# A recurrent stage rewritten as streams put in order by an account of the engines' time

## The chip, the cores and the metric

The kernel runs on one NeuronCore of one Trainium2 chip. The metric is device microseconds of that core. The kernel before took 2466.32 us, the median of 3 runs (2462.35 to 2467.48). The profiled execution took 2471.44 us, and its span, on which all rows below lie, is 2469.7 us.

## The reference, cut to what matters

Two attention blocks come first and are not touched. The second block is an RWKV-7 time mix beside a causal convolution, then an FFN. x is 512 tokens by 1024 features; there are 16 heads of 64.

```
proj = rms_norm(x) @ w_in                     # 1024 x 7168: r, k, v, conv value and gate, two z gates
r, k, v = lerp_shift(p_r), lerp_shift(p_k), lerp_shift(p_v)
decay, a, g = small LoRAs of the shifted h
for t in range(512):                          # wkv7, per head, S is 64 x 64
    S = S * w_t + (S @ a_t) b_t^T + v_t k_t^T
    y_t = S @ r_t
y_rwkv = (groupnorm(y) + bonus) * g  @ w_rwkv_out
c = u * sigmoid(gate);  c = sum over 31 taps of dw[t] * c[time - t]      # depthwise, causal
y_conv = silu(layer_norm(c)) @ w_conv_out     # the norm runs over all 1024 channels
merged = sigmoid(z_rwkv) * y_rwkv + sigmoid(z_conv) * y_conv
x = x + rms_norm(merged @ w_out);  x = x + rms_norm(ffn(rms_norm(x)))
```

## The kernel before, in words

Every large product is done with fp32 operands split into a high and a low fp32r part. A weight tile arrives in `raw` (512 KB, two buffers, SP queue), ScalarE copies the high part `wh` (L160), VectorE subtracts to the low part `wl` (L161), and TensorE runs 8 matmuls each of wh by hT_h (L274), wh by hT_l (L275) and wl by hT_h (L277), all 128x512. Such a set of 24 is a dense unit here. The stage that the change rewrites runs from about 1277 to 2049 us and holds 72 dense units (1728 matmuls of 128x512): 24 for r, k and v, 16 for the convolution's input, 16 for the gates, and 16 for the two output maps.

The recurrence is done in chunks of 64 tokens, for 8 pairs of heads. Two pairs make a group, so there are 4 groups. The steps are

- `pair_in`: the three projections of a pair, and its LoRAs (tile `lo`).
- `pair_out`: decays, key norms, the products of the two heads inside each chunk (L1024, 64 rows by 128 columns), and transposes to tokens (L1040). POOL does r to the power -1/2 (L883).
- `solve`: the inverse of 1 minus a lower triangle of 64, for 32 chunks of a group. VectorE does 15 dependent steps on blocks of 16 (L1093, L1095), in two halves; then TensorE joins blocks of 16 to 32 with two sets of 64 matmuls of 32x32 (L1107, L1113), joins 32 to 64 (L1123, L1130), and applies the result (L1143). Blocks go through HBM in between (`abd`, `ttd`), issued by POOL.
- `chain`: 8 chunks one after the other: two products of the state (L1160, L1169), copies (L1171 ScalarE, L1172 VectorE), the new state (L1176, then L1179 on VectorE with `ds` from POOL, L1165), and the rest of y (L1182). All are 64x64.
- `post`: group norm of y, bonus and gate (L1192 to L1211).

The convolution of a feature tile is 30 VectorE instructions in a row (L1228, the taps). Layer norm needs all 8 tiles.

The order in which the steps are called is written out (`ORD`, L1259), but the order on every engine is made by the Tile framework's scheduler, with hand-set priority offsets `O`. Every engine then runs its instructions in that fixed order.

In the rows, `p` is a PSUM bank, SV the state and its products, X and RA the chunk matrices, BKT keys by token.

Of the kernel before, what the change touches and what calls it, by code (L numbers as in the profile page):

```python
# [72 lines left out]
def _constants():  # L73
# [3 lines left out]
    blk = np.concatenate([same, i[:, None] % 32 < 16, i[:, None] % 32 == np.arange(32),  # L77
                          (i[:, None] == i[None, :]) - same / 64], 1).astype(np.float32)
# [7 lines left out]

@with_exitstack
def tile_two_blocks(ctx: ExitStack, tc: tile.TileContext, A, out):
    nc = tc.nc
# [7 lines left out]
    make_identity(nc, ident)  # L97
# [27 lines left out]
    W["n"] = 0  # L125

# [24 lines left out]
    def wload(src, a, b, views=None, into=None):  # L151

        raw = W["raw"].tile([P, a, b], F32, tag="raw", name="raw")
# [4 lines left out]
        h, l = into or wpair(a, b)  # L158
# [447 lines left out]
    with ExitStack() as es:  # L606
# [206 lines left out]
        blk = pm.tile([P, 2 * P + 33], F32, name="blk")  # L813
# [21 lines left out]
        ahead = [wload(wcols(A["w_in_2"][0], 0, KD, i * D, P), KD, P,  # L835
# [27 lines left out]
    with ExitStack() as es:  # L863
        es.enter_context(lows)
# [4 lines left out]
        nc.vector.memset(smask[:, ::C], 0.0)  # L869
        two = blk[:, :P:64]  # L870
        i32 = blk[:, P + 1 : P + 33]
        centre = blk[:, P + 33 :]
        BANKS.update(ps=[0, 1, 2], po=[3, 4, 5], ca=[6], cb=[7], cc=[6, 7])

        def col_rstd(sq, rhs, eps, op, expand, role="po", scale=1.0):

            ps = pst(role)
# [3 lines left out]
            r = cs.tile([P, 8], F32, tag="r8" + role, name="r8")  # L881
            nc.vector.tensor_scalar(r, ps[:, :8], eps, None, op)
            nc.gpsimd.tensor_tensor(r, r, neg_half.to_broadcast([P, 8]), ALU.pow)  # L883
            nc.scalar.activation(expand.rearrange("p (t h d) -> p t h d", t=NB, h=2),
                                 r.rearrange("p (t h) -> p t h", h=2)[:, :, :, None].to_broadcast([P, NB, 2, 64]), AF.Copy, scale=scale)
            ps = pst(role)
# [7 lines left out]
        with ExitStack() as es2:  # L894
            el = es2.enter_context(tc.tile_pool(name="el", bufs=1))

            SH = 1

            def et(tag, n=T, bufs=1):
                return el.tile([P, n], F32, tag=tag, name=tag, bufs=bufs)  # L900

            def shifted(src, scale=None, **kw):

                sh = el.tile([P, T + 2], F32, tag="sh", name="sh", bufs=SH)
                nc.gpsimd.memset(sh[:, 0:1], 0.0)
# [342 lines left out]
            def at(offset, f, *a):  # L1248

                if not offset:  # L1250
                    return f(*a)
# [161 lines left out]
```

## Time and profile before

| what | value |
|---|---|
| median of 3 runs | 2466.32 us |
| profiled execution, and its span | 2471.44 us, 2469.7 us |
| TensorE busy (PE) | 2377.3 us, 96% |
| VectorE (DVE), ScalarE (ACT), GpSimd (POOL) busy | 51%, 38%, 12% |
| stage 1277 to 2049 us: PE, DVE, ACT, POOL busy of 772 us | 730.8, 565.8, 343.1, 198.5 |
| mean granted TensorE clock in that stage | 0.94 of 2.4 GHz |

PE is TensorE, PEld its weight loads. A busy engine is not an engine at its peak: in the plain FFN stage TensorE passes 223 matmuls of 128x512 in 50 us, and what it passes in the recurrent stage has to be read against that. A row of matmuls gives the time until the last result, so consecutive rows overlap; the distance from one start to the next is the price.

### The profile page before, as it was taken

The numbers are of one execution on the slowest core, as the hardware profiler recorded it, in microseconds if no ns is written. First come the engines' busy times: TensorE is split into PE (matmuls) and PEld (weight loads), VectorE is DVE, ScalarE is ACT, GpSimd is POOL, SyncE is SP. The second block draws the span as 40 slices with busy tenths as digits, with TensorE's granted clock in tenths as the row PEclk, the third lists the DMA queues.
The fourth block names the chain that finished last, engine by engine and source line by source line (L and its number), as shares of the span: only waits on it lengthen the run. The fifth ranks groups of instructions, "written<-read, shape, count | busy, mean of one in ns | idle before, by whom it ended". The sixth has DMA issues, their size and how long they took to land. (4 is left out here: it accounts for less than half of the span.)

```text
span 2469.7 us, 34315 instructions
## 1 busy us (share of the span) xinstructions
PE 2377.3 (96%) x13667; PEld 1869.2 (76%) x13667; DVE 1250.3 (51%) x2083; ACT 934.9 (38%) x1681; POOL 287.2 (12%) x455
## 2 busy tenths in 40 slices
PE   7899999999999999999999899999989999999998
PEld 6756888888887788888886676666667777888887
DVE  4376532143434642223446877588587764422232
ACT  4365432142344542222346344444344343422231
POOL 1000120000100000000012223233142101000000
PEclk9999999999999999999999999899799999999999
DMA  7320763143542263332232222123125454533321
GB/s 202 107 77 35 217 185 98 55 134 106 154 120 79 65 184 96 94 102 93 70 91 82 76 90 71 60 72 92 54 80 174 124 171 148 162 96 95 100 95 60
DMA packets 294240, 263.39 MB, mean 107 GB/s; under 512 B 13904, under 2 KB 260756, under 8 KB 293696
## 3 DMA queue, kind: packets, MB, share of 16 engines
q1 hardware_dynamic: 274648, 208.82, 28.3%
q0 software_dynamic: 10352, 30.02, 3.8%
q10 hardware_dynamic: 9080, 22.37, 3.0%
q8 instruction: 107, 1.75, 0.3%
q14 instruction: 53, 0.43, 0.1%
HBM read 226.33 MB, written 34.83 MB: 106 GB/s over the span
## 5 line engine op out<-in xcount | busy, mean ns | idle before, releaser
L274 PE MATMUL p<-hT_h,wh 128*128 128x512 f32 (+1 forms) x1776 | 686.7, 391 | 7.0 <-DVE cc L1218 3.3
L275 PE MATMUL p<-hT_l,wh 128*128 128x512 f32 (+1 forms) x1776 | 685.7, 390 | 0.0
L161 DVE TENSOR_TENSOR wl<-raw,wh 128x1024 fp32r<-128x1024 f32 (+2 forms) x348 | 410.8, 1184 | 424.5 <-ACT wh L160 360.2
L160 ACT ACTIVATE wh<-raw 128x1024 fp32r<-128x1024 f32 (+2 forms) x348 | 352.2, 1015 | 633.9 <-PE p L275 418.9
L277 PE MATMUL p<-hT_h,wl 128*128 128x512 f32 (+1 forms) x1776 | 449.1, 388 | 7.7 <-DVE wl L161 7.7
L274 PEld LDWEIGHTS p<-hT_h,wh 128*128 128x128 f32 x1776 | 340.3, 192 | 75.4 <-DVE cc L1218 4.5
L275 PEld LDWEIGHTS p<-hT_l,wh 128*128 128x128 f32 x1776 | 340.2, 192 | 66.1 <-issue 2.5
L277 PEld LDWEIGHTS p<-hT_h,wl 128*128 128x128 f32 x1776 | 322.4, 190 | 73.2 <-DVE wl L161 8.1
L168 PE MATMUL p<-wh,fh 128*128 128x512 f32 x528 | 206.1, 390 | 1.5 <-ACT memv L376 0.8
L169 PE MATMUL p<-wl,fh 128*128 128x512 f32 x528 | 205.9, 390 | 0.0
L170 PE MATMUL p<-wh,fl 128*128 128x512 f32 x528 | 205.2, 389 | 0.0
L1228 DVE SCALAR_TENSOR_TENSOR acc<-c,dwc,acc 128x512 f32<-128x512 f32 x240 | 186.0, 775 | 4.5
L300 DVE TENSOR_TENSOR fT<-sg,p 128x384 f32<-128x384 f32 (+1 forms) x88 | 46.8, 552 | 258.7 <-PE p L277 249.5
L192 POOL TENSOR_SCALAR rstd<-ss 128x1 f32<-128x1 f32 x24 | 9.2, 383 | 1445.6 <-ACT junk L188 1445.5
L175 DVE TENSOR_TENSOR fl<-fT,fh 128x512 fp32r<-128x512 f32 x66 | 45.1, 691 | 144.4 <-ACT fh L174 144.4
L168 PEld LDWEIGHTS p<-wh,fh 128*128 128x128 f32 x528 | 99.1, 188 | 23.0 <-ACT memv L376 1.2
L169 PEld LDWEIGHTS p<-wl,fh 128*128 128x128 f32 x528 | 99.1, 188 | 20.3
L170 PEld LDWEIGHTS p<-wh,fl 128*128 128x128 f32 x528 | 99.1, 188 | 20.3
L174 ACT ACTIVATE fh<-fT 128x512 fp32r<-128x512 f32 x66 | 40.8, 628 | 182.7 <-PE p L169 174.8
L168 PE MATMUL p<-wh,hT_h 128*128 128x256 f32 (+1 forms) x256 | 91.7, 359 | 2.6 <-ACT v L536 2.0
L169 PE MATMUL p<-wl,hT_h 128*128 128x256 f32 (+1 forms) x256 | 90.2, 353 | 0.6 <-DVE wl L161 0.6
L170 PE MATMUL p<-wh,hT_l 128*128 128x256 f32 (+1 forms) x256 | 89.0, 351 | 0.0
(328 smaller groups left out, 3053.5 us busy)
## 6 DMA issues: line engine op xcount, KB each, us to landing
raw<-in_w_gu SPq DMA_DIRECT2D x88, 512.0 KB
raw<-in_w_in SPq DMA_DIRECT2D x56, 512.0 KB
raw<-in_w_down SPq DMA_DIRECT2D x44, 512.0 KB
raw<-in_ffn_w_gate SPq DMA_DIRECT2D x22, 512.0 KB
raw<-in_ffn_w_up SPq DMA_DIRECT2D x22, 512.0 KB
raw<-in_ffn_w_down SPq DMA_DIRECT2D x22, 512.0 KB
raw<-in_w_in_b SPq DMA_DIRECT2D x20, 512.0 KB
xs<-xt POOLq DMA_DIRECT2D x19, 512.0 KB, 4.0
```

The costliest lines, as they stand in the source:

```text
L160: nc.scalar.activation(to(h), fr(raw), AF.Copy)
L161: nc.vector.tensor_tensor(to(l), fr(raw), to(h).bitcast(F32), ALU.subtract)
L168: nc.tensor.matmul(ps, lhsT=lh, rhs=rh, start=start, stop=False)
L169: nc.tensor.matmul(ps, lhsT=lh, rhs=rl, start=False, stop=False)
L170: nc.tensor.matmul(ps, lhsT=ll, rhs=rh, start=False, stop=stop)
L174: nc.scalar.activation(h, src, AF.Copy)
L175: nc.vector.tensor_tensor(l, src, h.bitcast(F32), ALU.subtract)
L274: nc.tensor.matmul(o[:, c], lhsT=h[:, k, :], rhs=hT_h[:, k, c], start=k == 0, stop=False)
L275: nc.tensor.matmul(o[:, c], lhsT=h[:, k, :], rhs=hT_l[:, k, c], start=False, stop=False)
L277: nc.tensor.matmul(o[:, c], lhsT=l[:, k, :], rhs=hT_h[:, k, c], start=False, stop=k == KD - 1)
L300: nc.vector.tensor_tensor(dst(fT[:, f, :]), src(sg), src(ps[1]), ALU.mult)
L1228: nc.vector.scalar_tensor_tensor(acc, c[:, t : t + T], dwc[:, t, f : f + 1], acc, ALU.mult, ALU.add)
```

## The change

The stage's code is rewritten as Python generators. Each `yield` marks a point at which the next instruction would have to wait. `Clock` keeps an account of each engine's time from fixed costs per instruction; `drive` walks through the dense units and lets each stream (two `pair_out` streams at once, `solve`, `chain`, `post`, the layer norm) emit its next burst when the account says that its inputs are ready. Bursts other than plain continuations wait for every eighth matmul of a dense unit. `Taps` fills VectorE's accounted idle time with convolution taps. TensorE and VectorE keep exactly the order in which the code emits; ScalarE, POOL and SP are still ordered by the framework.

Beside the order: the solve starts from blocks of 8 (7 dependent steps on VectorE, whole 128 rows at once) and joins 8 to 16 and 16 to 32 on TensorE with six sets of 64 matmuls in place of two; its trips through HBM are issued by SP and not by POOL; every second weight subtraction of the stage goes to POOL (36 of them); raw weights are fetched two units ahead; the merged result goes to hT in place of its own tiles.

```diff
+class Clock:
...
+    def cost(self, engine, op, out, ins):
+        n = max(math.prod(x.shape[1:]) for x in [out, *ins])
+        if op == "dma_start":
+            return 0.65 if engine == "POOL" else 0.05
+        if engine == "DVE":
+            return (0.21 if op == "scalar_tensor_tensor" else 0.14) + n * (0.00215 if op.endswith("scan") else 0.00107)
+        if engine == "ACT":
+            return 0.17 + n * 0.00086
...
+    def op(self, engine, op, out, ins, f, a, k):
+        need = max([self.ready(x) + 0.25 for x in ins] + [self.read.get(self.name(out), 0.0)])
+        if engine == "DVE" and self.fill is not None and not self.filling:
+            self.filling = True
+            self.fill(need)
+            self.filling = False
+        start = max(self.t[engine], need)
+        end = self.t[engine] = start + self.cost(engine, op, out, ins)
...
+    def until(self, t):
+        busy, self.clock.filling = self.clock.filling, True
+        while not self.done and self.clock.free("DVE") + 0.75 <= t:
+            got = next(self.gen, None)
...
-            nc.vector.tensor_tensor(to(l), fr(raw), to(h).bitcast(F32), ALU.subtract)
+            W["sub"][W["n"] % len(W["sub"])].tensor_tensor(to(l), fr(raw), to(h).bitcast(F32), ALU.subtract)
...
+        W["sub"] = [nc.vector, nc.gpsimd]
...
-                parts = (slice(0, 64), slice(64, P)) if g >= HALF else (slice(0, P),)
-                for t in range(1, 16):
...
+            for t in range(1, 8):
+                p4 = pr[:, : 2 * t * t].rearrange("p (m j s) -> p m j s", m=2, s=t)
+                nc.vector.tensor_tensor(p4, tt[:, :, :t, :t], at[:, :, None, :t, t].to_broadcast([P, 2, t, t]), ALU.mult)
+                nc.vector.tensor_reduce(tt[:, :, :t, t], p4, AX.X, ALU.add)
...
+            de = s2("de")
+            nc.scalar.activation(de, quad(of(e), of(dt), True), AF.Copy)
+            yield BURST
+            pa, pb = quad(of(de), of(dd)), quad(of(dd), of(de))
...
+            de = s2("de")
+            nc.scalar.activation(de, quad(lambda i: diag[i], of(dt), True), AF.Copy)
+            yield BURST
+            pb, pa = quad(of(dd), of(de)), quad(of(de), of(dd))
...
+        def drive():
+            streams = [[s, 0.0, None] for s in (chains(), outs(0), outs(1), solves(), posts(), ends())]
+            def burst(minor=False):
+                for s in list(streams):
+                    while s[1] <= clock.free("PE") and not (minor and s[2] in (BURST, FREE)):
+                        before = clock.free("PE")
+                        clock.last = 0.0
+                        got = s[2] = next(s[0], "end")
...
+                for n, minor in enumerate(run(hl) if run is not None else ()):
+                    if n == SPLIT and more:
+                        nxt, more = units[i + 1][1](raws.pop(0)), False
+                    burst(minor)
+                    taps.until(clock.free("PE") - 1)
...
+        with tc.manual_schedule(engines={mybir.EngineType.PE, mybir.EngineType.DVE}):
+            drive()
```

Every instruction that the wrapper `Timed` passes on stands in the changed program under one of three lines (L185, L191 on TensorE, L151 elsewhere), so its tiles name it.

The first place is TensorE at the start of the last group's chain. Before (SV, X, BKT, RA belong to the recurrence, hT and w to a dense unit, bk to another pair's products):

```order
L275 MATMUL p_14117<-hT_l,wh 128x512
L277 MATMUL p_14117<-hT_h,wl 128x512
L1160 MATMUL p_13789<-SV_12582,X_12581 64x64
L277 MATMUL p_14117<-hT_h,wl 128x512
L1160 MATMUL p_13789<-SV_12582,X_12581 64x64
L277 MATMUL p_14117<-hT_h,wl 128x512
L1024 MATMUL p_14268<-X_14068,bk 128x128
L1160 MATMUL p_13789<-SV_12582,X_12581 64x64
L277 MATMUL p_14117<-hT_h,wl 128x512
L1024 MATMUL p_14268<-X_14068,bk 128x128
L1160 MATMUL p_13789<-SV_12582,X_12581 64x64
L277 MATMUL p_14117<-hT_h,wl 128x512
```

The same kind of place in the changed program, one chunk of a chain between two dense stretches:

```order
L191 MATMUL p_12852<-hT_h,wh 128x512
L191 MATMUL p_12852<-hT_l,wh 128x512
L191 MATMUL p_12804<-SV_10548,BKT_10549 64x64 x4
L191 MATMUL p_12805<-RA_11268,SV_10548 64x64 x4
L191 MATMUL p_12886<-blk,RA_10181 128x2 x4
L191 MATMUL p_12893<-blk,RA_10181 128x2 x4
L191 MATMUL p_12852<-hT_h,wh 128x512
L191 MATMUL p_12852<-hT_l,wh 128x512
```

The four matmuls of a step now stand together, where they stood singly between dense ones.

The second place is VectorE in a group's solve. Before, its last steps (pr and tt are the solve, SV the chain, wl a weight's low part):

```order
L1093 TENSOR_TENSOR pr<-tt,at 64x169 x2
L1095 TENSOR_REDUCE tt<-pr 64x13 x2
L1172 COPY SV_11129<-p_12500 64x2x64
L161 TENSOR_TENSOR wl<-raw,wh 128x128
L1093 TENSOR_TENSOR pr<-tt,at 64x196 x2
L938 SCALAR_TENSOR_TENSOR rkv<-p_13195,der,sh 128x512
L1179 TENSOR_TENSOR SV_11129<-p_12501,ds 64x2x64 x2
L1095 TENSOR_REDUCE tt<-pr 64x14 x2
L1093 TENSOR_TENSOR pr<-tt,at 64x225 x2
L161 TENSOR_TENSOR wl<-raw,wh 128x1024
```

Now, the end of the second group's (x is the solve's scratch tile):

```order
L151 TENSOR_TENSOR x<-x 128x50
L151 TENSOR_REDUCE x<-x 128x2x5
L151 TENSOR_TENSOR x<-x 128x72
L151 TENSOR_REDUCE x<-x 128x2x6
L151 TENSOR_TENSOR x<-x 128x98
L151 TENSOR_REDUCE x<-x 128x2x7
L151 TENSOR_TENSOR wl<-raw,wh 128x1024
L151 TENSOR_TENSOR SV_9906<-p_11720,ds 64x2x64 x2
```

A solve has 14 such instructions where it had 60, and they stand in one block with nothing between them.

The third place is TensorE where the last chain ends. Before, the group norm of the last group (RA with blk, then ysq) stands among the matmuls of the first output map (X, SV with wh):

```order
L277 MATMUL p_15729<-hT_h,wl 128x512 x8
L1192 MATMUL p_15758<-RA_14071,blk 128x512
L1192 MATMUL p_15785<-RA_14071,blk 128x512
L879 MATMUL p_15763<-blk,ysq 128x2 x4
L1314 MATMUL p_15814<-X_15220,wh 128x512
L1315 MATMUL p_15814<-SV_15221,wh 128x512
```

Now, the last two chunks and the group norm stand with nothing dense between them:

```order
L191 MATMUL p_16494<-hT_h,wl 128x512 x8
L191 MATMUL p_16541<-SV_13683,X_13682 64x64 x4
L191 MATMUL p_16542<-X_13682,SV_13683 64x64 x4
L191 MATMUL p_16541<-SV_13683,BKT_13684 64x64 x4
L191 MATMUL p_16542<-RA_14374,SV_13683 64x64 x4
L191 MATMUL p_16572<-SV_13683,X_13682 64x64 x4
L191 MATMUL p_16573<-X_13682,SV_13683 64x64 x4
L191 MATMUL p_16573<-RA_14374,SV_13683 64x64 x4
L191 MATMUL p_16592<-RA_14374,blk 128x512
L191 MATMUL p_16596<-RA_14374,blk 128x512
L191 MATMUL p_16604<-blk,RA_14374 128x2 x4
L191 MATMUL p_16612<-blk,RA_14374 128x2 x4
```

The dense work that lay beside these steps has moved ahead of them.

## Rows read from the trace of the kernel before

**Rows 1.** The page: the span, and busy time of each engine with its instructions
```profile
span 2469.7 us, 34315 instructions
...
PE 2377.3 (96%) x13667; PEld 1869.2 (76%) x13667; DVE 1250.3 (51%) x2083; ACT 934.9 (38%) x1681; POOL 287.2 (12%) x455
```

**Rows 2.** Windows: stretch, length, busy us (instructions) PE, PEld, DVE, ACT, POOL; clock, DMA
```profile
1277.00:2049.00 772.00, 730.79 (x5529) 525.68 (x5528) 565.83 (x1001) 343.10 (x624) 198.51 (x281) 0.94 0.32 95
...
2200.00:2250.00 50.00, 50.00 (x223) 41.38 (x222) 15.08 (x15) 12.54 (x14) 0.00 (x0) 1.00 0.33 95
```

**Rows 3.** Timeline of TensorE: start, duration, engine, line, one excursion from dense work
```profile
1902.18 0.40 PE L275 MATMUL p<-hT_l,wh 128*128 128x512 f32 x1
1902.51 0.33 PE L1182 MATMUL p<-RA,SV 64*64 64x64 f32 x2
1902.77 0.50 PE L274 MATMUL p<-hT_h,wh 128*128 128x512 f32 x1
1903.10 0.39 PE L275 MATMUL p<-hT_l,wh 128*128 128x512 f32 x1
```

**Rows 4.** Windows again: TensorE's clock before and after it fell
```profile
1736.20:1746.40 10.20, 10.20 (x149) 7.59 (x145) 6.29 (x12) 4.34 (x12) 2.95 (x3) 1.00 0.32 90
1746.50:1770.30 23.80, 23.80 (x78) 14.22 (x76) 9.57 (x17) 4.63 (x11) 1.46 (x3) 0.50 0.09 29
```

**Rows 5.** Timeline, all engines: TensorE stops for a weight behind a solve
```profile
1384.23 0.39 PE L275 MATMUL p<-hT_l,wh 128*128 128x512 f32 x1
...
1391.02 1.23 DVE L161 TENSOR_TENSOR wl<-raw,wh 128x1024 fp32r<-128x1024 f32 x1
```

**Rows 6.** Critical chain in the stage: start, duration, what
```profile
1277.27 1.81 PE p L277 x8
...
1392.31 3.78 PE p L277 x8
...
1555.37 2.00 PE p L1104 x2
1557.38 1.73 PE p L1107 x127
```

**Rows 7.** Lines of VectorE in the stage: count, busy us, mean ns, idle before, releaser
```profile
L1228 DVE SCALAR_TENSOR_TENSOR acc<-c,dwc,acc 128x512 f32<-128x512 f32 x240 | 186.0, 775 | 4.5
L161 DVE TENSOR_TENSOR wl<-raw,wh 128x1024 fp32r<-128x1024 f32 (+1 forms) x80 | 94.3, 1179 | 28.0 <-PE p L277 15.3 <-ACT wh L160 11.0 <-issue 1.1
L1093 DVE TENSOR_TENSOR pr<-tt,at 64x1 f32<-64x1 f32 (+14 forms) x120 | 38.5, 321 | 3.4
L1095 DVE TENSOR_REDUCE tt<-pr 64x1 f32<-64x1 f32 (+14 forms) x120 | 28.2, 235 | 3.6
```

**Rows 8.** Lines L1228, L1056 and L883: min/median/max ns
```profile
L1228 DVE SCALAR_TENSOR_TENSOR acc<-c,dwc,acc x240: 700/751/1784, 1351.8 to 1946.3; 128x512 f32<-128x512 f32 x120
...
L1056 POOL TENSOR_TENSOR rkv<-bk,D x16: 1037/1483/2561, 1304.2 to 1799.5; 128x512 f32<-128x512 f32 x16
...
L883 POOL TENSOR_TENSOR r<-r,neg_half x17: 1642/1717/2657, 1292.1 to 1981.0; 128x8 f32<-128x8 f32 x17
```

**Rows 9.** Timelines of POOL and VectorE around 1473 us, one tap beside two POOL products
```profile
1472.92 3.40 POOL L1056 TENSOR_TENSOR rkv<-bk,D 128x512 f32<-128x512 f32 x2 [0.26 <-DVE bk L1014]
...
1473.88 1.53 DVE L1228 SCALAR_TENSOR_TENSOR acc<-c,dwc,acc 128x512 f32<-128x512 f32 x1
```

**Rows 10.** Timeline of one step of a chain, from product to product
```profile
1911.38 0.45 PE L1169 MATMUL p<-X,SV 128*64 128x64 f32 x8
...
1911.92 0.27 ACT L1171 ACTIVATE SV<-p 64x128 f32<-64x128 f32 x1 [1.90 <-PE p L1169]
1912.28 0.29 DVE L1172 COPY SV<-p 64x128 f32<-64x128 f32 x1 [0.61 <-ACT SV L1171]
1912.42 0.32 PE L1182 MATMUL p<-RA,SV 64*64 64x64 f32 x2
```

**Rows 11.** Lines of POOL in the stage: one of the solve's four DMA issues
```profile
L1076 POOL DMA_DIRECT2D abd<-RA x16 | 10.6, 669 | 14.9 <-ACT RA L1031 11.7 <-ACT SV L1051 3.1
```

More of the change, by code (lines that the diff above doesn't have):

```diff
@@ new lines, in chunks, with dense @@
+        def chunks(t):
+            return t.rearrange("p (c t) -> p c t", t=C)
+        def dense(hl, xh=lambda k: hT_h[:, k, :], xl=lambda k: hT_l[:, k, :], cut=KD):
+            (h, l), ps = hl, pst()
+            n = 0
+            for ks in (range(cut), range(cut, KD)):
+                for part in range(2):
+                    for k in ks:
+                        if part:
+                            nc.tensor.matmul(ps, lhsT=l[:, k, :], rhs=xh(k), start=False, stop=k == KD - 1)
+                        else:
+                            nc.tensor.matmul(ps, lhsT=h[:, k, :], rhs=xh(k), start=k == 0, stop=False)
+                            nc.tensor.matmul(ps, lhsT=h[:, k, :], rhs=xl(k), start=False, stop=False)
+                        n += 2 - part
+                        if n % 2 == 0 and n < 3 * KD:
+                            yield n % 8 != 0
+            return ps
@@ new lines, in tile_two_blocks, with outs @@
+        nil = el.tile([64, 1024], F32, tag="bk", name="nil")
+        nc.gpsimd.memset(nil, 0.0)
+        for t in ttd:
+            DQ[10].dma_start(t.rearrange("p a b -> p (a b)"), nil)
+        def outs(jj):
+            for g in range(4):
+                j = 2 * g + jj
+                while not hasattr(pairs.get(j), "done") or chains_done < g - 1 or (jj and g not in groups) or L.decay:
+                    yield WAIT
+                L.decay = True
+                if jj == 0:
+                    groups[g] = group_tiles(g)
+                yield from pair_out(j, groups[g])
+                pairs[j].out = True
+                yield WAIT
@@ new lines, in solves, with enter_ln @@
+        def solves():
+            nonlocal solves_done
+            for g in range(4):
+                while not all(hasattr(pairs.get(2 * g + jj), "grams") for jj in range(2)):
+                    yield WAIT
+                yield from solve(g, groups[g])
+                solves_done += 1
+            enter_ln()
+        def enter_ln():
+            es2.close()
+            nonlocal lnp
+            lnp = es4.enter_context(tc.tile_pool(name="ln", bufs=1))
+            L.ct_h, L.ct_l = (cat(t[:, :4], t[:, 4:]) for t in (lnp.tile([P, KD, T], F32R, name=n) for n in ("ct_h", "ct_l")))
@@ L1373, in tile_two_blocks @@
+        taps = Taps(conv(), clock)
+        clock.fill = taps.until
+        clock.start()
+        with tc.manual_schedule(engines={mybir.EngineType.PE, mybir.EngineType.DVE}):
+            drive()
+        clock.on = False
+        es4.close()
+        W["sub"] = [nc.vector]
         with ExitStack() as es3:
```

1034 lines of the change are left out of this document (633 added, 401 removed).

## The prediction

> **What bounds the kernel now.** I read the page first: TensorE is busy for 2377 of 2470 us, no other engine for much over half [rows 1]. So TensorE sets the end, and the question is what it does in the stage that is rewritten. The windows answer that. In the stage, 772 us long, TensorE is without work for only 41 us (772 less 730.8) [rows 2]. But busy is not the same as passing work: the plain stage at 2200 us passes 223 large matmuls in 50 us, 0.224 us each [rows 2]; the recurrent stage has 72 dense units of 24, which at that price are 1728 x 0.224 = 387 us. Half of the stage is something else.
>
> I then went to the timeline for what a small product costs that stands between dense ones. From the dense start at 1902.18 to the dense start at 1903.10 are 0.92 us. Two dense matmuls are 0.45 of it, so one 64x64 product (two rows) costs 0.47 [rows 3]. Its own work is 0.04 to 0.1: eight rows last only 0.12 longer than two [rows 3, 10]. What is left, 0.37 to 0.43, is the price of leaving the full array and coming back. I take 0.37.
>
> Over the order of the stage, TensorE leaves products on the full 128x128 array for smaller ones 300 times before: 139 times into the chain's 128x64, 82 into 64x64, 34 into the 64-row products of two heads, 45 into LoRAs and 32x32. 300 x 0.37 = 111 us.
>
> The last part is the clock. Its mean over the stage is 0.94 [rows 2], so with two levels of 2.4 and 1.2 GHz about 12%, 93 us, ran at 1.2, which costs some 46 us.
>
> So the 772 us are 387 dense, 111 of leaving and returning, 46 clock, 41 idle, and 187 that remain for the small products' own work.
>
> **The change, part by part.**
>
> *Bursts on TensorE.* The same count over the changed order gives 96 trips in place of 300: the chain's four products of a step stand together, and several streams leave at the same point. 96 x 0.37 = 36 us, so 75 us go. At 0.43 it is 88; the lower bound is a gain of nothing, if the return costs by the product and not by the trip. Against that bound stand eight rows that cost 0.12 more than two.
>
> *The solve.* TensorE gets six sets of 64 small products per group instead of two, 16 sets more in all, and four more start-ups of L1104. The chain of waits prices a set at 1.73 us, and L1104 at 2.00 us at the low level, so 1.0 at the high one [rows 6]: 16 x 1.73 + 4 x 1.0 = 32 us. On VectorE 184 of 240 solve steps go, 0.278 us each (66.7 by 240) [rows 7]: 51 us. That removes one stop outright: TensorE stood from the end of the dense row at 1384.23 to 1392.31 for a weight whose subtraction came behind the solve, at 1391.02 [rows 5, 6].
>
> *Weights to POOL.* 36 subtractions leave VectorE, 36 x 1.18 = 42 us [rows 7], so VectorE falls from 566 us [rows 2] to about 473. On POOL a 128x512 product takes 1.04 us at least and 1.48 in the median [rows 8], so 128x1024 some 2.1 to 3.0, and POOL gains 75 to 108 us on 199 [rows 2]. Each is issued after a third of the dense unit before, and the low part is used in the last third of its own unit: 32 dense matmuls, 7 us, and the bursts between lie over it. I put it at nothing. If that cover went, it would be a late weight in every second unit, 1 us of each, 36 us.
>
> *Queues.* The solve's trips through HBM leave POOL (0.67 us each [rows 11]) and stand in SP's queue with the weights behind them. A raw weight is fetched two units ahead, some 11 us; the trip's read waits for the write before it. I price this at nothing, with a bound of 4 groups x 4 us.
>
> *The end of the recurrence.* The order shows the last chunks and the last group norm with nothing dense between. One step from product to product is 1911.38 to 1912.42 [rows 10], about 0.7 us beyond the products themselves; five such steps, then the power on POOL (1.72 [rows 8]) with its copies, then the norm's tail, of which the first 12 dense matmuls hide 2.7. I take 10 us, all of it new idle time.
>
> *What no row shows.* How far the account keeps step with the chip. TensorE runs strictly in the emitted order, so a wrong account shows as TensorE waiting. Bounds: only the 10 us above; or one whole tap held up by POOL (1.53 us [rows 9]) ahead of each of the 96 trips, 147 us. The nearest row is the stage as it is, 41 us, also a fixed order made from estimates. I take 40 with the 10 included, since the 8 us stop goes and a trip has more dense work ahead of it. The clock costs 0 to 46; fewer small pieces between dense ones should help, the bunched solves should not, and I take 18.
>
> A rule bears on that clock term. At 1746.5 the clock fell to 1.2 GHz for 23.8 us although TensorE was busy for all of the 10.2 us before, with 149 rows of small and large products in turn [rows 4]. The Trainium skill (TensorE: Matmul & The Clock Gate, "Why this matters for your kernels") ties drops in mid-kernel to gaps in which TensorE is idle. By that rule only the uncovered end would cost clock, some 5 us, and the sum below would be 13 us lower. The rows differ from it here, so I keep 18.
>
> Sum: 387 + 187 + 32 + 36 = 642 of work, + 40 + 18 = 700 us against 772, a gain of 72. From the profiled execution, 2471.4, that is 2399; the median lies 5 us lower, so 2394.
>
> **The rivals.**
>
> *The account slips a little.* TensorE waits 75 us, and the clock stays at 35: 642 + 110 = 752, a gain of 20, 2446. For it: fixed costs per instruction can't know what a queue holds. Against it: between two bursts there are mostly 8 dense matmuls, 1.8 us, and a chain's hop is 0.7.
>
> *VectorE behind its account (slower).* Taps are put into every gap that the account shows on VectorE, and the 36 new POOL subtractions hold VectorE. The row: a tap beside two POOL products took 1.53 us, where 0.70 is the least and 0.75 the median [rows 8, 9], so one 128x512 product holds it 0.78, one twice as wide 1.56; 36 of them hold it 56 us, more than the 42 that moving them saved. If all of that reaches TensorE through results that it waits for, idle is 96 and the clock stays at 46: 642 + 142 = 784, 12 more than before, 2478. It decides from 84 us of idle time, 0.88 us a trip; the 147 above would make it 2529. Against it: VectorE has 473 of 700 us to do, so it can catch up.
>
> The Trainium skill states the same (SBUF — State Buffer, "SBUF: two separate sides"): GpSimd and a VectorE instruction with two SBUF inputs hold a shared pair of ports in turn, and the loser is fully blocked. The 1.53 us agree with that. It is this rival's reason, and it speaks against the edit that moves subtractions to POOL.
>
> *More than that.* Idle only at the end and hardly any clock loss: 642 + 10 = 652, 2346.
>
> *It doesn't do what it says:* the order already shows the 96 trips, so I give this nothing.
>
> **How the numbers follow.** Forecast, 2345 to 2440: 0.70. A small gain, 2440 to 2461: 0.11. VectorE behind, 2461 and up: 0.15, of which 0.02 within 0.2% (5 us, about what a measurement of this kernel can tell from no change). More, under 2345: 0.04. So faster 0.85, same 0.02, slower 0.13. The range is 2345 to 2455: it leaves out the 0.04 below, the slower case and the last of the small gain, about 0.2 in all. The forecast's own range, from the bounds of idle and clock, is 2350 to 2440.
>
> **What would show it.** In the trace after, the stage from the first dense unit of the convolution's gate to the last merged tile should last near 700 us, with the products of a chain step next to each other and dense starts 0.23 us apart between trips. VectorE's solve should be 56 instructions of 0.2 to 0.4 us, POOL's subtractions 2 to 3 us each. TensorE's idle time should be under 60 us, with one piece near 10 us before the first output map. I am wrong if waits of TensorE on VectorE or POOL add up to over 80 us, if weights from POOL are late, or if the clock stays at 1.2 GHz through the solves.

## The result and the profile after

The changed kernel takes 2449.9 us in the median (2446.5 to 2455.0), beside 2464.7 of the kernel before: a ratio of 0.9944, 95% interval 0.9924 to 0.9965, so 0.6% or 15 us faster. 2394 was forecast. The direction is right; the gain of 72 us is not there.

The page of the changed kernel, as [rows 1] of before:

```profile
span 2453.2 us, 38288 instructions
...
PE 2319.7 (95%) x15723; PEld 1869.3 (76%) x15723; DVE 1191.4 (49%) x1846; ACT 953.1 (39%) x1721; POOL 347.3 (14%) x463
```

TensorE is busy for 58 us less, and the span is only 16.5 us shorter. The windows of the changed kernel, columns as in [rows 2]: the stage, and then the same time in three parts. The first has dense work to cover the recurrence, in the second only the last steps of the recurrence are left, the third is the output maps.

```profile
1280.00:2030.00 750.00, 669.92 (x7589) 523.89 (x7588) 505.90 (x764) 360.76 (x664) 258.14 (x281) 0.93 0.33 96
1280.00:1898.30 618.30, 558.18 (x7103) 437.12 (x7103) 422.65 (x658) 310.36 (x595) 226.47 (x266) 0.94 0.32 92
1898.30:1915.80 17.50, 11.00 (x86) 7.68 (x85) 13.03 (x22) 5.12 (x11) 5.02 (x4) 0.72 0.06 20
1915.80:2030.00 114.20, 100.74 (x406) 79.09 (x405) 70.22 (x86) 45.28 (x58) 26.66 (x11) 0.94 0.42 131
```

The same windows of the kernel before, where the first output map follows the last covering work almost at once:

```profile
1277.00:1946.00 669.00, 635.68 (x5110) 450.14 (x5109) 497.90 (x908) 296.41 (x564) 191.36 (x276) 0.93 0.29 86
1946.00:2049.00 103.00, 95.11 (x421) 75.54 (x421) 67.93 (x94) 46.69 (x62) 7.15 (x5) 1.00 0.52 157
```

The covered part gained 51 us (669 to 618.3). Then 17.5 come in that were not there, and the maps take 11 longer: 22 us are left. Two smaller losses outside the stage, 3 us ahead of it and 2.5 behind, were not followed up. TensorE stands for 80 us of the stage (750 less 669.9; before 41), and runs for 102 us at 1.2 GHz (mean 0.93; before 96), which costs 51. What it stands for, by the waits of TensorE in the stage (us, times, longest):

```profile
PE p L191 <- issue: 24.5, 11, 3.3
PE p L191 <- DVE wl L151: 14.6, 5, 7.9
PE p L191 <- DVE SV L151: 9.5, 8, 3.3
PE p L191 <- DVE rkv L151: 6.9, 4, 3.3
```

Of the 80 us, waits for results of VectorE are 43 in all, those for ScalarE 12. "issue" heads the list with 24.5: waiting that no semaphore explains. The timeline of TensorE shows where. One program matmul of 32x32 is two rows, so a set of 64 is 128:

```profile
1409.06 1.28 PE L191 MATMUL p<-dt,e 32*32 32x32 f32 x128
...
1411.18 1.24 PE L191 MATMUL p<-dd,de 32*32 32x32 f32 x123
1415.75 0.27 PE L191 MATMUL p<-dd,de 32*32 32x32 f32 x3 [3.33 <-issue]
...
1415.85 1.84 PE L191 MATMUL p<-de,dd 32*32 32x32 f32 x121
1419.50 0.32 PE L191 MATMUL p<-de,dd 32*32 32x32 f32 x5 [1.81 <-issue]
```

The engine stops in the middle of a set whose operands are all there. What it lacks is instructions. The page has a DMA queue of its own for them, q8; the transfers of that queue in this stretch, from the same trace:

```profile
q8 instruction: 123, 2.02, 0.3%
```

```
start 1405.52 us, took 1.26, 16384 bytes
start 1413.56 us, took 0.96, 16384 bytes
start 1416.88 us, took 1.16, 16384 bytes
start 1420.65 us, took 1.31, 16384 bytes
```

The page counts 123 such transfers; TensorE has 15723 matmuls and as many weight loads, 256 a transfer. One set of 64 is 128 matmuls and 128 loads: one whole transfer, used up in 1.3 us, while the transfers behind 1413.56 follow each other in 3.3 and 3.8 us, and nowhere in the trace do two start less than 3.3 apart. The matmuls resume 1.2 and 1.5 us after such a transfer has landed (1414.52 to 1415.75, 1418.04 to 1419.50); so do all 11 of the "issue" stops, 1.2 to 1.6 us after one.

The longest single stop, 7.9 us, has another cause. VectorE's timeline, and TensorE's row:

```profile
1854.01 0.69 DVE L151 TENSOR_TENSOR SV<-yv,X 128x512 fp32r<-128x512 f32 x1 [0.78 <-ACT X L151]
1854.62 6.05 DVE L151 SCALAR_TENSOR_TENSOR acc<-c,dwc,acc 128x512 f32<-128x512 f32 x5
1860.59 1.29 DVE L151 TENSOR_TENSOR BKT<-yv,X 128x512 fp32r<-128x512 f32 x2
...
1862.90 1.22 DVE L151 TENSOR_TENSOR wl<-raw,wh 128x1024 fp32r<-128x1024 f32 x1
```

```profile
1855.92 0.39 PE L191 MATMUL p<-hT_l,wh 128*128 128x512 f32 x1
1864.18 2.08 PE L191 MATMUL p<-hT_h,wl 128*128 128x512 f32 x4 [7.87 <-DVE wl L151]
```

posts() reads finished tiles back from HBM (yv) and splits them. These splits are written into VectorE's order right behind the issue of the loads; the account fills the wait for a load with taps, and the weight's low part, whose high part ScalarE had written by 1853.4, stands behind all of it. One of the five taps took 2.91 us instead of 0.75, beside a subtraction on POOL (the rows are with sub_dve below), so some 2.2 of the 7.9 us are POOL's.

The lines of VectorE and POOL, as [rows 7, 8]:

```profile
L151 DVE SCALAR_TENSOR_TENSOR acc<-c,dwc,acc 128x512 f32<-128x512 f32 x240 | 209.2, 873 | 7.1 <-ACT acc L151 0.9
L151 DVE TENSOR_TENSOR x<-x 128x2 f32<-128x2 f32 (+6 forms) x28 | 6.5, 233 | 3.8 <-DMA x<-abd 2.9
L151 DVE TENSOR_REDUCE x<-x 128x2 f32<-128x2 f32 (+6 forms) x28 | 5.5, 197 | 1.0
```

```profile
L151 POOL TENSOR_TENSOR wl<-raw,wh 128x1024 fp32r<-128x1024 f32 x39 | 97.6, 2504 | 151.6 <-PE p L191 51.4 <-ACT wh L151 29.6 <-issue 28.2
```

The solve fell from 66.7 to 12.0 us on VectorE. A tap became 98 ns longer in the mean, and POOL's 39 subtractions (the 36 counted ahead are those of the dense units) take 2.5 us each; no wait of TensorE is for one of them.

### The profile page after: what moved, and what is told of

Read it like the earlier page. It is cut to its first block, busy times and chain, and to the rows that moved or that the text cites. A ratio compares the mean times of both kernels' runs of the same rounds, so it can differ in the third digit from the quotient of the medians.

```text
span 2453.2 us, 38288 instructions
## 1 busy us (share of the span) xinstructions
PE 2319.7 (95%) x15723; PEld 1869.3 (76%) x15723; DVE 1191.4 (49%) x1846; ACT 953.1 (39%) x1721; POOL 347.3 (14%) x463
## 5 line engine op out<-in xcount | busy, mean ns | idle before, releaser
L185 PE MATMUL p<-hT_h,wh 128*128 128x512 f32 (+1 forms) x1376 | 511.5, 377 | 7.9 <-ACT qT L185 6.0
L185 DVE TENSOR_TENSOR wl<-raw,wh 128x1024 fp32r<-128x1024 f32 (+1 forms) x270 | 319.3, 1187 | 398.6 <-ACT wh L185 349.4
L185 PE MATMUL p<-hT_l,wh 128*128 128x512 f32 (+1 forms) x1376 | 511.1, 376 | 0.0
L185 ACT ACTIVATE wh<-raw 128x1024 fp32r<-128x1024 f32 (+1 forms) x270 | 275.9, 1026 | 548.8 <-PE p L185 374.1
L185 PE MATMUL p<-hT_h,wl 128*128 128x512 f32 (+1 forms) x1376 | 328.1, 376 | 0.0
L185 PEld LDWEIGHTS p<-hT_h,wh 128*128 128x128 f32 x1376 | 260.3, 189 | 56.1 <-ACT qT L185 6.4
L185 PEld LDWEIGHTS p<-hT_l,wh 128*128 128x128 f32 x1376 | 260.6, 189 | 46.7 <-issue 0.6
L185 PEld LDWEIGHTS p<-hT_h,wl 128*128 128x128 f32 x1376 | 248.4, 189 | 46.6 <-DVE wl L185 0.4
L185 POOL TENSOR_SCALAR rstd<-ss 128x1 f32<-128x1 f32 x52 | 17.7, 340 | 1460.2 <-ACT junk L185 1460.0
L151 DVE SCALAR_TENSOR_TENSOR acc<-c,dwc,acc 128x512 f32<-128x512 f32 x240 | 209.2, 873 | 7.1 <-ACT acc L151 0.9
L185 PE MATMUL p<-wh,fh 128*128 128x512 f32 x528 | 206.2, 390 | 1.6 <-ACT memv L185 0.9
L185 PE MATMUL p<-wl,fh 128*128 128x512 f32 x528 | 206.1, 390 | 0.0
L185 PE MATMUL p<-wh,fl 128*128 128x512 f32 x528 | 205.5, 390 | 0.0
L191 PE MATMUL p<-hT_h,wh 128*128 128x512 f32 x448 | 190.0, 424 | 0.7 <-ACT hn L185 0.7
L191 PE MATMUL p<-hT_l,wh 128*128 128x512 f32 x448 | 181.7, 406 | 0.0
L185 DVE TENSOR_TENSOR fT<-sg,p 128x384 f32<-128x384 f32 (+1 forms) x88 | 46.7, 552 | 257.0 <-PE p L185 250.4
L191 PE MATMUL p<-hT_h,wl 128*128 128x512 f32 x448 | 123.5, 420 | 7.9 <-DVE wl L151 7.9
L151 ACT ACTIVATE wh<-raw 128x1024 fp32r<-128x1024 f32 x78 | 77.2, 990 | 110.0 <-PE p L191 78.4
L151 POOL TENSOR_TENSOR wl<-raw,wh 128x1024 fp32r<-128x1024 f32 x39 | 97.6, 2504 | 151.6 <-PE p L191 51.4
L185 PEld LDWEIGHTS p<-wh,fh 128*128 128x128 f32 x528 | 99.2, 188 | 22.6 <-ACT memv L185 1.3
L185 DVE TENSOR_TENSOR fl<-fT,fh 128x512 fp32r<-128x512 f32 x66 | 45.1, 691 | 145.1 <-ACT fh L185 145.1
L185 PEld LDWEIGHTS p<-wl,fh 128*128 128x128 f32 x528 | 99.2, 188 | 20.5
```

Of the source, the lines that this page charges most:

```text
L151: return f(*a, **k)
L185: return f(*a, **k)
L191: return f(*a, **k)
```

## The experiments

The theory: the work went about as forecast; TensorE stands, and is then granted the low clock, because pairs of 32x32 sets outrun the supply of instructions, because a few results stand on VectorE behind others, and because the recurrence ends later than the work that covers it. The main rival: POOL's subtractions hold VectorE, and its lag is what TensorE waits for.

All against the kernel before, with 95% intervals; the last column is worked out from the ratio by 0.9944, in us of 2450, and uncertain by some 7.

| run | us | ratio | against the changed kernel |
|---|---|---|---|
| changed kernel | 2449.9 | 0.9944 (0.9924-0.9965) | |
| sets_apart | 2438.0 | 0.9899 (0.9880-0.9917) | -11 |
| one_of_pair | 2424.9 | 0.9846 (0.9826-0.9866) | -24 |
| sub_dve | 2468.3 | 1.0014 (0.9999-1.0030) | +17 |
| yv_late | 2439.8 | 0.9904 (0.9881-0.9926) | -10 |
| apart_yv | 2421.1 | 0.9822 (0.9793-0.9851) | -30 |
| apart_yv_tap | 2441.5 | 0.9892 (0.9865-0.9919) | -13 |
| apart_yv_pool | 2439.5 | 0.9885 (0.9856-0.9915) | -15 |
| apart_yv_eager | 2439.7 | 0.9890 (0.9860-0.9920) | -13 |
| spaced | 2453.8 | 0.9943 (0.9916-0.9969) | 0 |
| trip | 2524.9 | 1.0242 (1.0207-1.0278) | +73 |
| trip_once | 2459.3 | 0.9977 (0.9949-1.0005) | +8 |
| before_pool | 2530.4 | 1.0270 (1.0230-1.0309) | |
| after_less | 2456.0 | 0.9967 (0.9949-0.9986) | +6 |
| apart_less | 2422.1 | 0.9837 (0.9811-0.9863) | -26 |
| order_yv | 2423.5 | 0.9843 (0.9820-0.9866) | -25 |
| order_alone | 2453.9 | 0.9952 (0.9932-0.9971) | +2 |

**The sets of a pair apart (sets_apart).**

```diff
-            pa, pb = quad(of(de), of(dd)), quad(of(dd), of(de))
-            dd, dt = s2("dd"), s2("dt")
-            nc.vector.tensor_copy(dt, pb)
+            nc.vector.tensor_copy(dt, quad(of(dd), of(de)))
+            yield BURST
+            pa, dd = quad(of(de), of(dd)), s2("dd")
             nc.scalar.activation(dd, pa, AF.Copy)
```

(and the second pair in the same way)

> The two 32x32 sets of each pair in the solve are put into two bursts with dense matmuls between; the work is the same, 8 more trips. Theory (instruction supply: TensorE's instructions arrive in pieces of 16,384 bytes, and two sets in a row use them up faster than they come): the 24.5 us of idle time put down to issue fall to under 8, about half of the 37 us at 1.2 GHz that follow these gaps go, and the run is 20 to 30 us shorter, 2420 to 2430. Rival (VectorE behind its account, held by POOL's subtractions): the issue gaps are not what costs, some move elsewhere, and the run stays within 5 us of 2450 or is 3 us longer for the trips.

Waits of TensorE in its stage, four of the list:

```profile
PE p L191 <- DVE rkv L151: 10.3, 6, 3.3
PE p L191 <- DVE wl L151: 9.3, 3, 8.2
PE p L191 <- DVE ssum L151: 8.6, 1, 8.6
PE p L191 <- issue: 8.4, 6, 3.0
```

Issue fell from 24.5 to 8.4 us with every instruction still there, as the theory wants. The time fell by 11 and not by 20 to 30: new waits for the convolution's norm (8.6 us for ssum, 6.6 for asum), now behind the last covering work, took most of the rest.

**One set of each pair left out (one_of_pair).**

```diff
-            pa, pb = quad(of(de), of(dd)), quad(of(dd), of(de))
+            pa = pb = quad(of(de), of(dd))
```

> Leaves out the second set of each of the 8 pairs; one product serves as both results. Theory (instruction supply): the sets' own 8 x 1.3 us, nearly all of the 24.5 us of issue idle and 10 to 18 us of clock go, 45 to 50 us in all, about 2402. Rival (the sets cost their own work only, the idle time is set elsewhere): 8 x 1.3 = 10 us, about 2440.

2425: 24 us less, between the two. The sets' own 10 us and 14 more; issue fell to 4.8. Waits for other results grew (rkv from 6.9 to 12.1), and the time at 1.2 GHz fell by only 10 us, which is 5 where 10 to 18 were expected.

**Subtractions back on VectorE (sub_dve).**

```diff
-        W["sub"] = [nc.vector, nc.gpsimd]
+        W["sub"] = [nc.vector]
```

> All subtractions of weights back on VectorE, everything else as changed. Rival (POOL's 39 subtractions hold VectorE): taps fall from 873 ns to about 780, TensorE's waits on VectorE fall from some 45 us to under 25, the run is 15 to 40 us shorter. Theory (issue gaps and a few in-order waits): VectorE gets 42 us more of work in a stage where it is busy for 524 of 750, and little changes: within 8 us either way of 2450, the 24.5 us of issue idle stay.

Neither: 17 us slower. Its tap line, and its waits:

```profile
L151 DVE SCALAR_TENSOR_TENSOR acc<-c,dwc,acc 128x512 f32<-128x512 f32 x240 | 185.1, 772 | 6.4
```

```profile
PE p L191 <- issue: 21.2, 10, 3.1
PE p L191 <- DVE ssum L151: 10.4, 1, 10.4
PE p L191 <- POOL asum L151: 9.1, 1, 9.1
```

The rival's mechanism is real. Taps are 101 ns shorter without POOL beside them, 24 us over 240, or 0.62 us for each of the 39 subtractions. That mean hides how it goes: most taps take the same 752 ns in both kernels, and a few stand for nearly a whole subtraction. Rows of the changed kernel:

```profile
L151 DVE SCALAR_TENSOR_TENSOR acc<-c,dwc,acc x240: 629/752/2911, 1295.1 to 1926.3; 128x512 f32<-128x512 f32 x120
1855.41 2.36 POOL L151 TENSOR_TENSOR wl<-raw,wh 128x1024 fp32r<-128x1024 f32 x1
1855.40 2.91 DVE L151 SCALAR_TENSOR_TENSOR acc<-c,dwc,acc 128x512 f32<-128x512 f32 x1
```

The tap ends 0.55 us behind the subtraction. So do all 16 taps that were held by one, whether they began with it or 2.2 us into it. Other instructions of VectorE are held too; a subtraction met a held instruction 26 times in 39. Each instruction beside a subtraction, less the median of its kind, makes some 40 us in all (an estimate from the trace). Moving the subtractions saves VectorE 39 x 1.28 = 50 us (1284 ns is the mean of one there). So VectorE's work hardly changes: in sub_dve it is busy for 513.9 us of the stage, in the changed kernel for 505.9.

```profile
1280.00:2040.00 760.00, 673.02 (x7592) 524.78 (x7591) 513.85 (x804) 361.88 (x665) 154.16 (x236) 0.92 0.33 95
```

In sub_dve 19.5 us of the convolution's norm stand uncovered. The edit also gives the account another price for each subtraction, so the order is another one; how much of the 17 us comes from the order and how much from VectorE's own work was not separated. The edit that the rival speaks against is worth about as much as the whole net gain of the change; what the holds cost TensorE beside that is not known, as no run is without both the holds and the 50 us.

**The splits after their loads (yv_late).**

```diff
                         nc.sync.dma_start(yv, yd[f])
+                        yield
                         split(L.yT_h(f), L.yT_l(f), yv)
```

> The six splits of the stored normed tiles are emitted after the account's end of each load instead of right behind its issue. Theory (one in-order wait: TensorE stood 7.9 us at 1856.3 for a low weight part that stood on VectorE behind taps and the split of a tile still loading): that gap and the 6.8 us at 1.2 GHz behind it go, 8 to 11 us, about 2440. Rival (VectorE is late in general): the wait moves to the next result of VectorE, under 4 us of change.

10 us less, and the waits for wl fell from 14.6 to 3.6: as the theory has it.

**Both (apart_yv).**

> Both edits together: the two sets of each pair apart, and the splits of the stored tiles after the account's end of their loads. Theory (two separate stops of TensorE): the gains add, 11 and 9 from about 2449, so 2424 to 2434. Rival (VectorE's taps end too late for the convolution's norm, as in sets_apart, where TensorE then stood 8.6, 3.6 and 3.0 us in that norm): the time won comes back as waiting in the norm, 2436 to 2441.

2421, 1.8% or some 44 us below the kernel before: the fastest kernel here. Its windows in the same three parts:

```profile
1280.00:1859.00 579.00, 544.94 (x7096) 427.86 (x7094) 428.53 (x660) 306.87 (x592) 229.74 (x262) 0.96 0.34 98
1859.00:1891.10 32.10, 14.91 (x95) 10.00 (x95) 23.89 (x40) 12.78 (x23) 6.53 (x6) 0.63 0.08 27
1891.10:1994.00 102.90, 96.03 (x394) 76.26 (x394) 52.76 (x63) 38.10 (x47) 23.56 (x10) 0.95 0.47 140
```

The covered part gained another 39 us, and 15 of them came back as 32 us without cover, of which 10.4 are a wait for the sum of the convolution's norm. A covered part of 579 us, 90 below before, is what the prediction had in mind; the rest is the tail that it had priced at 10.

**The price of a tap in the account (apart_yv_tap, apart_yv_eager).** The 0.21 of Clock.cost for a tap becomes 0.32 in the one and 0.14 in the other.

> As apart_yv, and the account prices a tap of the convolution at 0.87 us, as measured, in place of 0.76. Theory (what is left of TensorE's waits on VectorE comes from an account that runs ahead of VectorE): these waits, some 30 us, fall by half, and the run is 8 to 15 us shorter than apart_yv. Rival (VectorE's amount of work sets when the taps end, whatever the account says): within 4 us of apart_yv, and the waits before the convolution's norm stay.

> As apart_yv, and the account prices a tap at 0.69 us in place of 0.76 (0.87 is measured), so that it puts more of them into VectorE's gaps. Theory (the taps' end sets when the convolution's norm starts, and what of the norm stands behind the last cover is lost): norm 10 us or more earlier, the 10.4 us of waiting before its sum mostly gone, 5 to 12 us shorter than apart_yv. Rival (VectorE runs behind its account and TensorE pays): waits on SV, rkv and RA, 24 us in apart_yv, grow by 10 or more, as long as apart_yv or longer.

Both theories fall: by the ratios 17 us slower than apart_yv with the price that was measured, and 17 slower with a lower one. With 0.87 the norm's sum comes at 1933 in place of 1879, behind the first output maps; with 0.69 TensorE waits 9.5 us for that sum (10.4 in apart_yv) and 9.5 more, which are new, for the first tile of the last group.

**All subtractions on POOL (apart_yv_pool).**

```diff
-        W["sub"] = [nc.vector, nc.gpsimd]
+        W["sub"] = [nc.gpsimd]
```

> As apart_yv, with every subtraction of weights in the stage on POOL, 78 instead of 39. Theory (VectorE's amount of work sets the end of the taps): each saves VectorE 1.25 us and slows its taps by some 0.6, so VectorE has 25 us less to do, and the run is 5 to 15 us shorter than apart_yv. Rival (POOL, 78 x 2.5 = 195 us of them, is late with weights): TensorE waits for wl on POOL before many dense units, 10 us slower or more.

15 us slower than apart_yv, and not for the rival's reason: TensorE waited for VectorE's RA (12.5 us), SV (12.1) and acc (9.3), hardly for wl. It doesn't test the theory either, since VectorE's work did not fall by 25 us:

```profile
1280.00:2014.00 734.00, 666.04 (x7595) 520.49 (x7593) 498.78 (x731) 362.66 (x665) 338.84 (x314) 0.93 0.34 98
```

VectorE is busy for 498.8 us, 6 less than in apart_yv (505.2, the sum of its three parts), with 39 subtractions fewer; its taps went from 880 to 953 ns in the mean.

**Sets spaced (spaced).** After a set, that stream's next step starts 3.0 us later at the earliest by the account.

```diff
+                        if clock.quad > quad:
+                            s[1] = max(s[1], clock.quad + 3.0)
```

> As apart_yv, and the account lets no set of 32x32 products follow another in under 3.0 us. Theory (instruction supply, a piece of 256 instructions each 3.3 to 3.8 us): the 9.0 us of issue idle that are left fall to under 3, and the run is 5 to 12 us shorter than apart_yv. Rival (the solve, now longer, holds up the chain behind it): the issue idle goes, but as much comes back before the chain or the norm; within 4 us.

```profile
PE p L191 <- ACT X L151: 9.6, 1, 9.6
...
PE p L191 <- issue: 3.1, 4, 1.6
```

Issue fell to 3.1 us as expected. The run got 30 us longer than apart_yv all the same: the norm came before the last group's own end, and TensorE stood 9.6 us for that group's first tile in the middle of an output map. The rest of the 30 was not followed up. Removing a stop is worth nothing if the order that follows from it ends worse.

**The price of a trip (trip, trip_once).** 64-column products on the full array put into the chain.

```diff
+            def full(ps):
+                tc.nc.tensor.matmul(ps[:, 256:320], lhsT=ident, rhs=ident[:, 0:64], start=True, stop=True)
```

> The changed kernel with 64 products on the full array, 64 columns each, put into the chain between its 128x64 products and its 64x64 ones (results unused, the order else the same): 157 trips off the full array in place of 96. Prediction's price (0.37 us a trip): 61 x 0.37 + 64 x 0.05 = 26 us more, 2475. Rival (the cost is by the product and not by the trip): 64 x 0.05 = 3 us, 2452; in between, if idle time takes up part of it.

> As trip, but only the 32 products between the chain's first two groups, which wait for nothing that the groups around them don't wait for: 128 trips in place of 96. Prediction's price: 32 x (0.37 + 0.05) = 13 us more than the changed kernel, about 2463, and no wait of TensorE before them. Rival (a trip costs over 1 us, as the 75 us of trip by 61 would have it): 35 us or more, 2485.

trip came out at +73, three times the expectation, because half of its products do wait:

```profile
PE p L1431 <- DVE SV L151: 48.4, 29, 5.1
```

The second of each step is written behind the addition to SV and was made to wait for it. Of the 67 us between the two profiled spans (2520.6 and 2453.2), 26 are idle time (84 to 110), 26 are clock (106 to 157 us at 1.2 GHz), and 16 are left, 0.25 for each of 64. The first of each step has no such wait; a timeline of trip, and the same place in a step of the changed kernel:

```profile
1460.27 0.45 PE L191 MATMUL p<-SV,X 128*64 128x64 f32 x8
1460.65 0.43 PE L1431 MATMUL p<-ident 128*128 128x64 f32 x2
1461.01 0.45 PE L191 MATMUL p<-X,SV 128*64 128x64 f32 x8
```

```profile
1898.23 0.45 PE L191 MATMUL p<-SV,X 128*64 128x64 f32 x8
1898.51 0.40 PE L191 MATMUL p<-X,SV 128*64 128x64 f32 x8
```

From the start of the one group to the start of the other it is 0.74 us with the product and 0.28 without, so 0.46 for the product and the way there and back. trip_once, with these alone, is 8 us longer (13 expected; the intervals allow 0 to 17); its profiled span is 3 us longer, with 4 less of idle time and 7 less of clock, so 14 of work, 0.42 each. Three readings from 0.25 to 0.46, the product's own 0.05 included: the forecast's 0.37 and 0.05 lie among them.

**POOL's subtractions in the kernel before (before_pool).** As sub_dve the other way round, W["sub"] in the stage alone.

> The kernel before with every second subtraction of weights in the stage on POOL, nothing else. Theory (VectorE's amount of work counts where the taps' end is on the path, as in the changed kernel, where the same edit is worth 19 us): in the kernel before the end of the stage has cover, so within 8 us either way. Rival (POOL's subtractions hold VectorE by as much as they take from it): taps go from 775 to 870 ns or more and the run is 10 us longer or more.

67 us slower. Its tap line and stage:

```profile
L1230 DVE SCALAR_TENSOR_TENSOR acc<-c,dwc,acc 128x512 f32<-128x512 f32 x240 | 197.3, 822 | 10.9 <-ACT acc L1227 6.3
```

```profile
1277.00:2094.00 817.00, 749.61 (x5518) 537.91 (x5517) 570.22 (x955) 339.28 (x622) 282.63 (x319) 0.91 0.30 90
```

Taps at 822 ns are only 11 us. But VectorE as a whole is busy for 570 us, before for 566 [rows 2], though its weight subtractions fell by 44 us (94.3 [rows 7] to 50.7): POOL's hold it by about as much as they take, as the rival has it. TensorE's idle time went from 41 to 67 us and its time at 1.2 GHz from 96 to 147, and the scheduler's order of TensorE is another one. How much of the 67 us is the holds and how much the order stays open.

**Covering work taken away (after_less, apart_less).**

```diff
+                if i and f > 4:
+                    ps = pst()
+                    nc.tensor.matmul(ps, lhsT=hl[0][:, 0, :], rhs=hT_h[:, 0, :], start=True, stop=False)
+                    nc.tensor.matmul(ps, lhsT=hl[1][:, 0, :], rhs=hT_h[:, 0, :], start=False, stop=True)
+                else:
+                    ps = yield from dense(hl)
```

> The changed kernel with three of the 16 gate projections cut to 2 of their 24 large matmuls (66 matmuls, 66 x 0.224 = 15 us of TensorE's covering work left out; their outputs are then wrong). Theory (the recurrence's own last steps set when the first output map starts, TensorE has 17.5 us there without cover): under 6 us shorter, the stretch without dense work grows by as much as was left out. Rival (TensorE's work still sets the end): 13 to 18 us shorter.

> The same cut in apart_yv, where the stretch without dense work is 32 us. Theory (recurrence sets the end): within 5 us of apart_yv, 2421. Rival (TensorE's work sets it): 13 to 18 us shorter, about 2406.

15 us of TensorE's work less, and no time won in either: +6 against the changed kernel (0.9967 beside 0.9944, the intervals overlap), +1 against apart_yv. The edit takes more than work away: a unit of two matmuls has one point at which a stream may emit where a whole one has 12, and leaves less time for the next weight. The windows of after_less:

```profile
1280.00:1886.40 606.40, 543.27 (x6954) 425.86 (x6952) 407.79 (x635) 306.52 (x589) 217.16 (x256) 0.92 0.32 91
1886.40:1915.00 28.60, 18.02 (x166) 13.45 (x165) 21.38 (x35) 8.27 (x18) 11.66 (x12) 0.56 0.24 75
```

The first output map starts at 1915.0, as in the changed kernel (1915.8); the uncovered part grew from 17.5 to 28.6, and 4.5 us of waiting for the low parts of the shortened units' weights are new. So in the changed kernel TensorE's amount of work does not set by itself when the maps start; the recurrence, as it is ordered, does.

This does not carry over to apart_yv. There the last 10.4 of the 32 us are a wait for the sum of the convolution's norm, which VectorE makes. In apart_less that sum comes behind the first maps, and they start 12.7 us earlier (1878.4 beside 1891.1), though the shortened units waited 6.6 us for low parts. Two of its rows:

```profile
1843.68 0.80 PE L191 MATMUL p<-hT_h,wl 128*128 128x512 f32 x1 [4.28 <-POOL wl L151]
1878.44 0.78 PE L191 MATMUL p<-X,wh 128*128 128x512 f32 x1
```

The maps then take 18 us longer, so nothing is won.

Nor does the recurrence run at its own pace. In the changed kernel its last steps under cover follow each other in 7.3 us, one to a dense unit (1890.96 to 1898.23); in after_less, without cover, in 3.4 (1898.73 to 1902.13). An order that puts the last steps closer together was not tried.

**The last pairs earlier (order_yv, order_alone).**

```diff
-        for what in ("c0 i0 i1 c1 i2 i3 c2 c3 i4 c4 i5 c5 i6 c6 i7 c7 "
+        for what in ("c0 i0 i1 c1 i2 i3 c2 i4 c3 i5 c4 i6 i7 c5 c6 c7 "
```

> As apart_yv, and the inputs of pairs 4 to 7 stand one unit of the convolution earlier in the list of dense work (c2 i4 c3 i5 c4 i6 i7 c5 c6 c7 in place of c2 c3 i4 c4 i5 c5 i6 c6 i7 c7). Theory (recurrence sets the end): the recurrence starts its last steps under cover, the stretch without dense work falls from 32 to under 20 us, the run is 8 to 18 us shorter than apart_yv. Rival (the convolution's taps, now later, set it): waits before the convolution's norm and maps grow by as much, no gain or a loss of up to 10.

> The changed kernel with only that other order of the list, no other edit. Theory (recurrence sets the end): the 17.5 us without dense work fall to under 10, 5 to 12 us shorter than the changed kernel, about 2440. Rival (the taps' end sets it): the convolution's norm is late, 2450 or more.

Windows of order_yv:

```profile
1280.00:1890.70 610.70, 559.01 (x7176) 439.68 (x7176) 446.26 (x686) 314.06 (x606) 227.43 (x265) 0.94 0.32 94
1890.70:1997.00 106.30, 95.66 (x400) 75.67 (x399) 66.04 (x76) 43.78 (x56) 27.02 (x12) 0.97 0.45 139
```

The uncovered part is gone (32 us to nothing), and not one us is won: the first map starts at 1890.3, in apart_yv at 1891.1. The covered part is 32 us longer, with 52 us of idle time in it instead of 34 and 72 us at 1.2 GHz instead of 41: what stood in the tail (17 and 24) now stands before it. order_alone is no faster than the changed kernel, and its uncovered part is 19.9, of which 10.6 are for the norm's sum. So a tail under cover is not a tail saved: in order_yv TensorE waits 12.9 us for VectorE's rkv, 11.9 for SV and 7.6 for RA, where apart_yv has 8.0, 9.4 and 6.4. What it would take to shorten these waits was not tried.

## Why the prediction was wrong

*Work, 642 forecast.* 750 less 80 idle and 51 clock is 619: the term was right in kind and 23 us too high. 7 of them are the sets: 1.73 each was read at the low clock [rows 6], and 16 more at 1.28 are 7 us less. The trip's price is about right (0.25 to 0.46, against 0.42 with the product's own work). Where the other 16 are from was not settled. Bursts, solve and trips did what they were to do. The 23 us hide part of the 73 that idle time and clock took beyond the forecast.

*Idle time, 40 forecast, 80 found.* This is the step that failed: "The nearest row is the stage as it is, 41 us, also a fixed order made from estimates. I take 40 ... since the 8 us stop goes and a trip has more dense work ahead of it." Twice that came, and 32 of the 40 us more by two causes that no term had. Bunching the small products, which saves the trips, makes runs of 256 matmuls and as many weight loads that the supply of instructions can't follow: 24.5 us. The rows of before held a hint: a set of 64 is 128 rows there too [rows 6], but the sets stood apart; two stops of this kind, 1.9 us at L1113, are in its trace. And the part "Queues" looked for late transfers among the solve's; it was the loads of finished tiles that cost 7.9 us, through VectorE's order, and 2.2 of it through POOL's hold on a tap, not through the queue. The runs bear both out: sets_apart and yv_late took 11 and 10 us off, both together 30.

*Clock, 18 forecast, 51 found.* In before, TensorE fell to 1.2 GHz 12 times in the stage: 5 times (31 us) just behind a stop of 1.9 us or more, and 7 times (65 us) without one, as in [rows 4]. In the changed kernel it fell 19 times (102 us), each time behind a stop of 1 us or more. So "fewer small pieces between dense ones should help" fits: the 65 us are gone, though no run shows that the fewer pieces did it. The stops made new ones. The Trainium skill (TensorE: Matmul & The Clock Gate, "Why this matters for your kernels") ties drops in mid-kernel to idle gaps. All 19 here stand behind one, but 13 of these stops are shorter than the gaps it warns of, and the 7 of before stand behind none of 1 us. The prediction weighed it against the 10 us of the end alone; the changed kernel has 69 us of idle time in 28 stops of 1 us or more. The mean spell behind a stop is 5.4 us, 2.7 us of loss, as much as the stop itself.

*The end.* 10 us forecast. 17.5 came, with 6.5 idle and 9.8 at the low clock, and the maps behind it are 11 longer (13.5 us idle beside 7.9, 14 us at 1.2 GHz beside none). The step counted TensorE's idle time only, not the low clock, and not that a covered part which gets faster uncovers more of a recurrence whose steps stay where the order put them.

*VectorE behind its account.* The rival's price was 1.56 us for each POOL subtraction, 56 in all; it is some 40 in all, 23 of them in the taps, against 50 saved. The hold itself is longer than the price (2.2 us for the tap at 1855.40), but 13 of the 39 subtractions met nothing that they held. The Trainium skill's shared ports (SBUF — State Buffer, "SBUF: two separate sides") show here as it has them, the instruction that comes second stands until the first is done: the 16 held taps all end 0.55 us behind POOL's subtraction. Of TensorE's 80 us of idle time 43 are for VectorE and 0.2 for POOL, where this rival decides from 84. What came is nearest the rival "the account slips a little", 2446, in the part of the chances that got 0.11: 80 us idle where it has 75, with 51 of clock for 35, and less work.

*What held.* VectorE's solve is 56 instructions of 0.15 to 0.36 us. Weights from POOL are in time. The 8 us stop of [rows 5, 6] is gone.

## What to carry to other kernels

A saving in the busy time of the engine that sets the end is worth what its waits leave of it: ask of each burst how fast its instructions are used up, of each in-order wait what stands behind it, and count a stop twice where the clock falls behind it (2.7 us of loss for a mean stop of 2.75 here). When covering work gets faster, look at what it covered, and at where the order puts its steps: here 15 us less of that work won nothing. And a written-out order is one of many that are nearly alike; a small price in its account moved this kernel by 15 to 30 us, so an edit to it is worth only what a run says.

## What the runs showed of the hardware that was not expected

- TensorE's instructions arrive in transfers of 16384 bytes, 256 instructions each. When it uses them up faster, the next start 3.3 to 3.8 us apart, and it stands up to 3.3 us within a row of matmuls, with "issue" as the only sign. Putting the two sets of a pair apart took this from 24.5 to 8.4 us.
- A tap (two operands in SBUF) that begins while POOL subtracts (2.4 us for 128x1024) stands until 0.55 us behind POOL's end, 2.91 us instead of 0.75 at the most. A VectorE instruction with an operand in PSUM did not: rkv<-p took 0.75 us at 1396.92, within a subtraction that ran from 1396.20 to 1398.60.
- So moving 39 subtractions to POOL took 50 us from VectorE and gave some 40 back.
- A product on the full array between two of the chain's groups cost 0.46 us (0.74 from group to group where it was 0.28).
